# Two reorderings in a hybrid decoder layer: the differences of the second MLP weights two behind a product, and the first small products of head 0 twenty multiplications later

## The chip, the cores and the metric

The kernel runs on one core of one Trainium2 chip. The metric is the device time of one execution in microseconds (us). Before the change it is 1800.55 us, the median of three timed runs (1799.66, 1800.55 and 1804.9).

## The reference

One decoder layer in float32, sequence 1024, width 1024. A token mixer runs two branches side by side, sliding-window attention and a gated delta rule with eight heads; both are gated, added, projected and normalized. A squared-ReLU MLP with 4096 hidden channels follows. The parts that the change touches:

```python
u2 = x * (1.0 + sc2) + sh2
h = jnp.square(jax.nn.relu(u2 @ w_ff1[l] + b_ff1[l]))
x = _layer_norm(ALPHA * x + (1.0 + gt2) * (h @ w_ff2[l] + b_ff2[l]), ln2_g[l], ln2_b[l])
```

and, in the delta rule, for each head a triangular solve by chunks (`lax.linalg.triangular_solve(a_mat, rhs, ...)`), which the kernel does with an explicit inverse made of 64x64 blocks.

## The kernel before

**Numbers.** Every float32 factor of the large products is split into a high part (a copy on ScalarE, ACT, line 207) and a low part (raw minus high on VectorE, DVE, line 208). A product of two such factors takes three TensorE (PE) multiplications per block: high by high, high by low, low by high. One multiplication here is one MATMUL of 128x128 by 128x512.

**Order.** One list of events sets the order. `at(p, f)` puts a step at position p, where a position counts the large multiplications issued so far; before each multiplication all steps due by its position are emitted, those of equal position in the order in which they were put in. `after(n, f)` means n multiplications after the present one. PE, DVE and ACT run what was emitted in exactly that order. An engine doesn't wait for a position: it runs its next instruction as soon as its inputs are there and its output is free. POOL (GpSimd) and SP only issue DMAs in the stages below; their order is set by the framework.

**First MLP product.** It starts at position F0. The 2x2 blocks of `u2 @ w_ff1` are made with seven products instead of eight (names 1 to 7, table PROD), for 16 pairs of weight columns, i = 0 to 15. One product is 12 multiplications, so that 112 products make 1344 multiplications (line 2206). From pair 6 on a pair's order is 1, 2, 6, 5, 7, 3, 4. Products 1, 6, 7 and 4 add into one PSUM bank (tag `mm`; for pairs 3 and 4 tag `b`). After products 1 and 6 ACT copies the bank out (line 1920); after product 7 DVE adds it to a tile in SBUF (`full`, line 1389, emitted one multiplication after the product's end), and product 4 may not write to the bank before that has ended. Between product 7 and product 4 lies only product 3 (from pair 6 on; in the first pairs another one of 12 multiplications).

**What else DVE does there.** For each pair it makes sums and differences of the first weights (`f_sums`, `f_sums2`: tiles `x` and `fraw`), the low parts `wl` and `wd` (line 208), sums of the hidden activations (`h_sums`, `h_sums2`: tiles `sa`, `t` and `sb`), and the `full` additions (`t<-t,mm`, `t<-t,a`, `t<-t,b`).

**Differences of the second weights.** The second MLP product uses the same scheme, and needs four differences of blocks of `w_ff2` for each of 16 pairs n. `t_load(n)` issues three loads on POOL, 40 positions ahead (lines 2024 to 2026): into both halves of a tile `one`, into the first half of a tile `two`, and into one half of a tile `sb`. These tiles are single: the loads for pair n + 1 wait until pair n's results have been written out. `t_make(n)` at `F0 + MAKE[n]` does four subtractions on DVE in a row (tiles `wx`, `wx`, `wx`, `sb`; 128x512 each) and issues four DMAs on POOL that write the results to DRAM (line 2036). They are read again in the second MLP product, the last stage (multiplications of line 2266).

**Head 0.** The delta rule's heads start with `hd_load(h)` at position `early`, which loads the head's data; for head 0 it also issues `hd_solved(0)`: four loads on SP (lines 1140, 1141) into the single tiles `L21` and `T1`. `hd_z(0)` is eight PE products of 64x64 of these two tiles (line 1186) and a copy of the result to `Z` on ACT (line 1187). `hd_solved(1)` then loads head 1's blocks into the same two tiles, so that these four loads, on SP, wait for the products of `hd_z(0)`. `hd_x(0)` uses `Z` (line 1196) and is followed at once by `hd_z(1)`, which needs head 1's `L21` and `T1`.

Of the kernel before, what the change touches and what calls it, by code (L numbers as in the profile page):

```python
# [34 lines left out]
def hybrid_layer_kernel(ctx: ExitStack, tc: tile.TileContext,  # L35
                        x, c, w_ada, b_ada, w_in, conv_w, a_log, dt_bias, sinks, dn_norm_w,
                        w_oa, w_ob, w_out, ln1_g, ln1_b, w_ff1, b_ff1, w_ff2, b_ff2,
                        ln2_g, ln2_b, out, dbg=None):
    nc = tc.nc
    x, c, out = x[0], c[0], out[0]  # L40
# [6 lines left out]
    V, A, G, T = nc.vector, nc.scalar, nc.gpsimd, nc.tensor  # L47
# [40 lines left out]
    wt_d = dram.tile([4, D_FF // (2 * P), P, HALF], F32, name="wt_d")  # L88
# [100 lines left out]
    def at(p, f, *args):  # L189
        order[0] += 1  # L190
        heapq.heappush(events, (p, order[0], f, args))

    def after(n, f, *args):
        at(count[0] + n, f, *args)
# [357 lines left out]
    with tc.tile_pool(name="pa", bufs=2, side="right") as pa:  # L552
        if True:
            ba = pv.tile([P, NT, 16], F32, name="ba")
            for t in range(NT):
# [14 lines left out]
                if t:  # L570
                    vd = pa.tile([P, 4, 64], F32, tag="vd", name="vd", bufs=1)
                    a, b = (vraw, pv4) if t % 2 == 0 else (pv4, vraw)
# [101 lines left out]
        for h in range(8):  # L674
# [7 lines left out]
            for half in range(2):  # L682
                tp = psum("c", 1) if half else psum("b", 2)
                for j in range(4):
                    n = 4 * half + j
                    T.transpose(tp[:, j * P:(j + 1) * P], kT[:, n * P:(n + 1) * P], ident)
                for j in range(4):
                    n = 4 * half + j
# [16 lines left out]
            for half in range(2):  # L705
                kk = psum("a", 2)
                for j in range(4):
                    n = 4 * half + j
                    kc = kT[:, n * P:(n + 1) * P]
                    T.matmul(kk[:, j * P:(j + 1) * P], lhsT=kc, rhs=kc, start=True, stop=True)  # L710
                for j in range(4):
                    n = 4 * half + j
# [646 lines left out]
    for h in range(8):  # L1359
        R = R0 + PER * h  # L1360
        early = max(R - 118, OPEN + 1)
        at(early, hd_load, h)
        for half in range(2):
            at(R - 45 + 15 * half, hd_kq, h, half)
            at(R - 40 + 15 * half, hd_qturn, h, half)
            at(R - 10 + 15 * half, hd_vturn, h, half)
            at(R + (122 + 8 * half if h < 7 else 100 + 5 * half), hd_silu, h, half)
        if h == 0:
            at(early + 50, hd_z, 0)
            at(early + 52, hd_solved, 1)  # L1370
        at(R - 55 if h else R0 - 30, hd_x, h)
        at(R + 35, hd_gate, h)
        for n in range(NT):
            at(R + 3 * HOP * n, hd_a, h, n)
            at(R + 3 * HOP * n + HOP, hd_b, h, n)
            at(R + 3 * HOP * n + 2 * HOP, hd_c, h, n)
        at(R + PER + 2, hd_norm, h)
        at(R + PER + (45 if h < 7 else 29), hd_out, h, 0)
        at(R + PER + (60 if h < 7 else 33), hd_out, h, 1)
# [5 lines left out]
    def sub(E, out, a, b):  # L1385
        E.tensor_tensor(out=out, in0=a, in1=b, op=ALU.subtract)
# [256 lines left out]
    F0 = E0 + 4 * SEG  # L1643
# [313 lines left out]
    def half_s(j):  # L1957

        if "s" not in sums_:
            sums_["s"] = big2.tile([P, 2, HALF], F32, tag="l7", name="sb")  # L1960
        return sums_["s"][:, j]
# [30 lines left out]
    for i in range(1, NPAIR):  # L1992
        if i < EARLY:
            b = pos[i, 5]
# [6 lines left out]
        else:  # L2001
            b = pos[i, 1]
# [25 lines left out]
    def t_make(n):  # L2028
        one, two = wpair[n]
        t1, t2, t3, t4 = one[:, 0], two[:, 0], two[:, 1], half_s(1)  # L2030
        sub(V, t1, one[:, 1], t1)
        sub(V, t3, t2, one[:, 1])
        sub(V, t2, t2, t1)
        sub(V, t4, t4, t2)
        for j, t in enumerate((t1, t2, t3, t4)):
            nc.gpsimd.dma_start(out=wt_d[j, n], in_=t)

    MAKE = (172, 246, 320, 394, 484, 552, 620, 693, 767, 842, 916, 990, 1068, 1139, 1214, 1288)
    for n in range(NPAIR):
        at(F0 + MAKE[n] - 40, t_load, n)  # L2040
        at(F0 + MAKE[n], t_make, n)

# [146 lines left out]
    for i, m in seq:  # L2191
# [8 lines left out]
        for k in range(4):  # L2200
            for x_ in range(3):
# [3 lines left out]
                a, b = ((wh, uh_), (wh, ul_), (wl, uh_))[x_]  # L2205
# [139 lines left out]
```

## Time and profile before

| | before |
|---|---|
| timed runs, median of 3 | 1800.55 us (1799.66 to 1804.9) |
| profiled execution | 1801.69 us |
| its span, first to last instruction | 1800.0 us |
| PE busy | 99% of the span |
| DVE, ACT, POOL busy | 72%, 58%, 18% |
| granted TensorE clock, mean | 0.998 |
| DMA, mean | 195 GB/s |

All times in rows are from one profiled execution, in us from its first instruction. A row of the timeline gives start, duration, engine, line, operation, output and inputs, the count of merged instructions, and in brackets how long the engine stood idle just before and what released it. A busy share of 99% does not say that PE is at its peak: multiplications are pipelined, each is shown for 0.39 us, and the next starts 0.23 us after it. What an idle gap costs is therefore read from the starts of neighbouring multiplications.

### The profile page before, as it was taken

To read this page: it belongs to the slowest core of one execution; us is meant where nothing else is said; L and a number is where in the kernel's file an instruction comes from. 1 tells how busy PE (TensorE), PEld (TensorE's weight loads), DVE (VectorE), ACT (ScalarE), POOL (GpSimd) and SP (SyncE) were. 2 spreads that over 40 slices of the span, in tenths; PEclk is the share of its full clock that TensorE was granted. 3 is DMA by queue.
4 is the path that set the end of the run, shared out by engine and by line. 5 is a ranking of instruction groups with operands and counts; after the bars stand their busy time and mean duration, and the time that the engine had idled before them with its cause. 6 is when DMAs were issued, how large, how long until landed. Compare 5 with 4: busy or idle time off the path is not lost.

```text
span 1800.0 us, 26327 instructions
## 1 busy us (share of the span) xinstructions
PE 1781.7 (99%) x9134; PEld 1499.0 (83%) x9134; DVE 1303.5 (72%) x2411; ACT 1043.1 (58%) x2368; POOL 323.6 (18%) x478
## 2 busy tenths in 40 slices
PE   8999999999999999999999999999999999999998
PEld 6888888888888888888888888888888888888887
DVE  7677688988855576766687455888777766676697
ACT  4699678888865565655474341475555454434341
POOL 0333234554331011111002210002122120000000
PEclk9999999999999999999999999999999999999999
DMA  9555822232256565665747644359888889665571
GB/s 329 169 202 195 227 77 90 66 106 78 79 206 192 160 171 171 172 184 179 237 154 274 203 130 164 129 189 324 291 284 270 279 289 392 236 192 184 207 260 47
DMA packets 254295, 350.32 MB, mean 195 GB/s; under 512 B 26345, under 2 KB 158130, under 8 KB 253906
## 3 DMA queue, kind: packets, MB, share of 16 engines
q1 hardware_dynamic: 212146, 220.78, 38.4%
q0 software_dynamic: 31488, 106.85, 17.6%
q10 hardware_dynamic: 10528, 21.00, 3.2%
q8 instruction: 72, 1.18, 0.3%
q14 instruction: 61, 0.50, 0.1%
HBM read 238.74 MB, written 107.75 MB: 192 GB/s over the span
## 4 chain that ended last, share of the span: by engine, by line
PE 84%; ACT 5%; DVE 4%; DMA 2%; issue 1%; POOL 1%; ACTq 0%; SPq 0%; DVEq 0%; POOLq 0%
PE mm L250 33%; PE mm L2206 8%; PE mm L2266 7%; PE a L2266 4%; PE b L2206 4%; PE b L2266 4%; PE a L2206 3%; PE mm L1611 2%; PE c L2266 2%; PE c L933 2%; PE mm L1835 1%; PE b L1611 1%; PE a L859 1%; PE a L858 1%; PE a L1835 1%
## 5 line engine op out<-in xcount | busy, mean ns | idle before, releaser
L250 PE MATMUL mm<-uh,wh 128*128 128x512 f32 x800 | 319.7, 400 | 0.0
L250 PE MATMUL mm<-uh,wl 128*128 128x512 f32 x800 | 319.6, 400 | 0.0
L250 PE MATMUL mm<-ul,wh 128*128 128x512 f32 x800 | 318.8, 399 | 0.0
L208 DVE TENSOR_TENSOR sp<-sraw,sp 128x1024 fp32r<-128x1024 f32 x112 | 132.8, 1220 | 75.6 <-ACT sp L207 75.4
L207 ACT ACTIVATE sp<-sraw 128x1024 fp32r<-128x1024 f32 x112 | 112.6, 1053 | 121.0 <-PE b L2266 75.4
L250 PEld LDWEIGHTS mm<-uh,wh 128*128 128x128 f32 x800 | 150.7, 188 | 26.3 <-issue 0.2
L250 PEld LDWEIGHTS mm<-ul,wh 128*128 128x128 f32 x800 | 150.8, 188 | 26.0
L250 PEld LDWEIGHTS mm<-uh,wl 128*128 128x128 f32 x800 | 150.8, 188 | 26.0
L2266 PE MATMUL mm<-sp 128*128 128x512 f32 x528 | 135.9, 389 | 0.0
L2266 PEld LDWEIGHTS mm<-sp 128*128 128x128 f32 x528 | 98.8, 188 | 20.3
L2266 PE MATMUL a<-sp 128*128 128x512 f32 x336 | 92.2, 389 | 0.0
L1282 ACT ACTIVATE vn<-a,brk 128x128 f32<-128x128 f32 x64 | 23.6, 369 | 110.9 <-PE a L1280 110.9
L866 DVE CUSTOM_DVE_ANT_0 nscore<-a,amask,nsink 128x256 f32<-128x256 f32 (+1 forms) x128 | 54.4, 462 | 37.9 <-PE a L859 37.6
L225 DVE TENSOR_TENSOR wl<-wr,wh 128x1024 fp32r<-128x1024 f32 x56 | 72.7, 1298 | 11.2 <-ACT wh L221 11.0
L2266 PE MATMUL b<-sp 128*128 128x512 f32 (+1 forms) x336 | 79.6, 374 | 0.0
L877 POOL TENSOR_TENSOR sm<-sm 128x256 f32<-128x256 f32 x56 | 56.4, 1007 | 105.2 <-ACT sm L873 80.1
L2266 PEld LDWEIGHTS a<-sp 128*128 128x128 f32 x336 | 63.1, 188 | 13.1
L2266 PEld LDWEIGHTS b<-sp 128*128 128x128 f32 x336 | 60.3, 188 | 11.2
L208 DVE TENSOR_TENSOR wl<-fraw,wh 128x1024 fp32r<-128x1024 f32 x43 | 52.5, 1222 | 19.7 <-ACT wh L207 19.6
L207 ACT ACTIVATE wh<-fraw 128x1024 fp32r<-128x1024 f32 x43 | 44.9, 1055 | 31.0 <-PE b L2206 25.0
L873 ACT ACTIVATE sm<-nscore,stat 128x257 f32<-128x257 f32 (+1 forms) x128 | 61.9, 487 | 1.0 <-DVE stat L866 0.8
L756 DVE TENSOR_TENSOR stt<-M 128x62 f32<-128x62 f32 (+30 forms) x62 | 58.8, 949 | 2.7 <-issue 2.4
(566 smaller groups left out, 4737.1 us busy)
## 6 DMA issues: line engine op xcount, KB each, us to landing
wr<-in_w_in_dram SPq DMA_DIRECT2D x60, 512.0 KB, 3.6
sraw<-hf_d SPq DMA_DIRECT2D x54, 512.0 KB, 3.8
adaw<-in_w_ada_dram SPq DMA_DIRECT2D x83, 256.0 KB, 5.2
fraw<-in_w_ff_dram SPq DMA_DIRECT2D x32, 512.0 KB, 5.3
sraw<-wt_d SPq DMA_DIRECT2D x32, 512.0 KB, 4.3
hf_d<-t ACTq DMA_DIRECT2D x48, 256.0 KB, 4.3
wt_d<-wx POOLq DMA_DIRECT2D x48, 256.0 KB, 4.1
sraw<-in_w_ff_dram SPq DMA_DIRECT2D x22, 512.0 KB, 4.8
```

What stands on the lines that cost most here:

```text
L207: A.activation(out=hi, in_=src, func=AF.Copy)
L208: after(lag, lambda: V.tensor_tensor(out=lo, in0=src, in1=hi.bitcast(F32), op=ALU.subtract))
L225: V.tensor_tensor(out=hl[1], in0=raw, in1=hl[0].bitcast(F32), op=ALU.subtract)
L250: T.matmul(ts[half], lhsT=w[:, k, :], rhs=xx[k][:, sl], start=k == 0 and m == 0, stop=k == KT - 1 and m == 2)
L756: V.tensor_tensor(out=tv, in0=bc(M[:, 0:s, s:s + 1], [P, s, w]), in1=bc(M[:, s:s + 1, s + 1:64], [P, s, w]), op=ALU.mult)
L866: V.tensor_tensor_reduce(out=ns[:, i, 1:1 + W], in0=sc[:, i * 2 * P:i * 2 * P + W], in1=amask[:, mo:mo + W], scale=-1.0, scalar=nsink[:, 2 ...
L873: A.activation(out=sm[:, i, 0:1 + W], in_=ns[:, i, 0:1 + W], func=AF.Exp, scale=-1.0, bias=st[:, i:i + 1], accum_out=st[:, 2 + i:3 + i])
L877: G.tensor_tensor(out=sm[:, :, 1 + P:1 + 2 * P], in0=sm[:, :, 1:1 + P], in1=sm[:, :, 1 + P:1 + 2 * P], op=ALU.add)
L933: T.matmul(av[:, 0:256], lhsT=vt[:, b, :], rhs=p_[:, m, :], start=p_ is full and m == 0, stop=p_ is prods[-1][1] and m == 1)
L1611: T.matmul(pt, lhsT=t[:, lw, k, :], rhs=r[:, k % 2, :], start=begin and k == 0 and x_ == 0, stop=k == 3 and x_ == 2, skip_group_check=True)
L2206: T.matmul(pt, lhsT=a[:, kk, :], rhs=b[k], start=begin and k == 0 and x_ == 0, stop=k == 3 and x_ == 2, skip_group_check=True)
L2266: T.matmul(to, lhsT=a[:, f, t * P:(t + 1) * P], rhs=b[:, f, lo:up], start=(begin or own) and s % NS == 0 and f == 0 and x_ == 0, stop=s % ...
```

## The change

Two things move, and nothing is added or left out.

1. The four subtractions of `t_make` become two groups of two. The first group (`t1`, `t3`) is emitted two multiplications behind the end of a product, the second (`t2`, `t4`) twelve later, again two behind the end of a product. Each subtraction is followed by its own write to DRAM. `MAKE` stays, and is rounded: 172 becomes 170, 246 becomes 242, 394 becomes 398, 1068 becomes 1070. `t_load` stays where it was.
2. `hd_z(0)` is emitted at `early + 70` in place of `early + 50`. `hd_solved(1)` stays at `early + 52`, so that it now stands ahead of it.

```diff
         if h == 0:
-            at(early + 50, hd_z, 0)
+            at(early + 70, hd_z, 0)
             at(early + 52, hd_solved, 1)
@@
     def t_make(n):
         one, two = wpair[n]
         t1, t2, t3, t4 = one[:, 0], two[:, 0], two[:, 1], half_s(1)
-        sub(V, t1, one[:, 1], t1)
-        sub(V, t3, t2, one[:, 1])
-        sub(V, t2, t2, t1)
-        sub(V, t4, t4, t2)
-        for j, t in enumerate((t1, t2, t3, t4)):
-            nc.gpsimd.dma_start(out=wt_d[j, n], in_=t)
+        for j, (t, a, b) in enumerate(((t1, one[:, 1], t1), (t3, t2, one[:, 1]), (t2, t2, t1), (t4, t4, t2))):
+            after(12 * (j // 2), t_one_sum, n, (0, 2, 1, 3)[j], t, a, b)
+
+    def t_one_sum(n, j, t, a, b):
+        sub(V, t, a, b)
+        nc.gpsimd.dma_start(out=wt_d[j, n], in_=t)
...
         at(F0 + MAKE[n] - 40, t_load, n)
-        at(F0 + MAKE[n], t_make, n)
+        at(F0 + (MAKE[n] + 4) // 12 * 12 + 2, t_make, n)
```

The order on DVE at weight pair n = 12, before the change. `wx<-wx x3` and `sb<-sb,wx` are the four subtractions; `t<-t,mm` is the addition after product 7 of column pair 12, for which product 4 waits:

```order
L1386 TENSOR_TENSOR fraw<-fraw 128x512 x2
L208 TENSOR_TENSOR wl<-fraw,wh 128x1024
L1386 TENSOR_TENSOR wx<-wx 128x512 x3
L1386 TENSOR_TENSOR sb<-sb,wx 128x512
L1389 TENSOR_TENSOR t<-t,mm 128x512
L208 TENSOR_TENSOR wd<-x,wd 128x512
L1389 TENSOR_TENSOR t<-t,b 128x512
L208 TENSOR_TENSOR wl<-fraw,wh 128x1024
```

The same place in the changed kernel:

```order
L1386 TENSOR_TENSOR fraw<-fraw 128x512 x2
L208 TENSOR_TENSOR wl<-fraw,wh 128x1024
L1389 TENSOR_TENSOR t<-t,mm 128x512
L1386 TENSOR_TENSOR wx<-wx 128x512 x2
L208 TENSOR_TENSOR wd<-x,wd 128x512
L1389 TENSOR_TENSOR t<-t,b 128x512
L1386 TENSOR_TENSOR wx<-wx 128x512
L1386 TENSOR_TENSOR sb<-sb,wx 128x512
L208 TENSOR_TENSOR wl<-fraw,wh 128x1024
```

All four subtractions stood ahead of `t<-t,mm`; now none does.

The order on DVE at n = 3, among the first column pairs, as a piece of the difference. `t<-t,b` is the addition for which product 4 of column pair 4 waits:

```order
 L1386 TENSOR_TENSOR fraw<-fraw 128x512 x2
 L1386 TENSOR_TENSOR sb<-t,sa 128x512
-L1386 TENSOR_TENSOR wx<-wx 128x512 x3
+L1389 TENSOR_TENSOR t<-t,a 128x512
+L1386 TENSOR_TENSOR wx<-wx 128x512 x2
+L1389 TENSOR_TENSOR t<-t,b 128x512
+L1386 TENSOR_TENSOR wx<-wx 128x512
 L1386 TENSOR_TENSOR sb<-sb,wx 128x512
-L1389 TENSOR_TENSOR t<-t,a 128x512
-L1389 TENSOR_TENSOR t<-t,b 128x512
 L208 TENSOR_TENSOR wd<-x,wd 128x512
```

Four subtractions stood ahead of both additions; now none stands ahead of the first of them, and two ahead of the second.

The order on DVE at n = 8, before the change. `sa<-t`, `t<-t`, `sa<-t` are `h_sums` of column pair 8, `x<-fraw` and the three `fraw` rows behind it the sums of the first weights:

```order
L1386 TENSOR_TENSOR wx<-wx 128x512 x3
L1386 TENSOR_TENSOR sb<-sb,wx 128x512
L1386 TENSOR_TENSOR sa<-t 128x512
L1389 TENSOR_TENSOR t<-t 128x512
L1386 TENSOR_TENSOR sa<-t 128x512
L208 TENSOR_TENSOR wl<-fraw,wh 128x1024
L1386 TENSOR_TENSOR sb<-t,sa 128x512
L1389 TENSOR_TENSOR t<-t,a 128x512
L1386 TENSOR_TENSOR x<-fraw 128x512
```

The same place in the changed kernel:

```order
L1386 TENSOR_TENSOR sa<-t 128x512
L1389 TENSOR_TENSOR t<-t 128x512
L1386 TENSOR_TENSOR sa<-t 128x512
L208 TENSOR_TENSOR wl<-fraw,wh 128x1024
L1386 TENSOR_TENSOR wx<-wx 128x512 x2
L1386 TENSOR_TENSOR sb<-t,sa 128x512
L1389 TENSOR_TENSOR t<-t,a 128x512
L1386 TENSOR_TENSOR wx<-wx 128x512
L1386 TENSOR_TENSOR sb<-sb,wx 128x512
L1386 TENSOR_TENSOR x<-fraw 128x512
```

The subtractions stood ahead of `h_sums`; now they stand behind them and the `wl` row, and all four still ahead of `x<-fraw`.

On PE the eight products of `hd_z(0)` stand twenty large multiplications later, and on ACT the copy to `Z` stands behind one more `pad` copy, `vT` copy and `vT` activation. On SP the four loads of `hd_solved(1)` keep their place among the other DMAs; they wait for those eight products, as before. The order on POOL is the same.

## The prediction

> **What bounds the kernel now.** I read the page's totals first, then what PE waits for, then the timeline at those places.
>
> ```profile
> PE 1781.7 (99%) x9134; PEld 1499.0 (83%) x9134; DVE 1303.5 (72%) x2411; ACT 1043.1 (58%) x2368; POOL 323.6 (18%) x478
> ```
>
> PE is busy 99% of the span, so work that moves on DVE, ACT or the queues is worth what PE's waiting on it costs, no more. The waits of PE in the first MLP product (1155 to 1480 us), with what it waited for, total, times and longest:
>
> ```profile
> PE mm L2206 <- DVE t L1389: 0.8, 1, 0.8
> PE b L2206 <- DVE t L1389: 0.5, 1, 0.5
> PE c L2206 <- ACT t L1920: 0.2, 1, 0.2
> PE c L2206 <- DVE wl L208: 0.2, 1, 0.2
> ```
>
> Two waits for the addition `t` on DVE, two small others, and nothing else in 300 us. What the two cost is read from the starts of multiplications; undisturbed, 24 take 5.44 us, 0.227 each. Here is the multiplication ahead of each wait and the one that waited, for the first also the next:
>
> ```profile
> 1220.18 5.44 PE mm L2206 x24
> 1274.19 0.39 PE L2206 MATMUL mm<-u11h,wl 128*128 128x512 f32 x1
> 1275.10 0.50 PE L2206 MATMUL b<-mh,wh 128*128 128x512 f32 x1 [0.52 <-DVE t L1389]
> 1275.44 0.39 PE L2206 MATMUL b<-ml,wh 128*128 128x512 f32 x1
> 1424.92 0.39 PE L2206 MATMUL b<-u22h,wl 128*128 128x512 f32 x1
> 1426.11 0.50 PE L2206 MATMUL mm<-mh,wh 128*128 128x512 f32 x1 [0.80 <-DVE t L1389]
> ```
>
> First wait: 1275.44 - 1274.19 = 1.25 for two steps that take 0.45, 0.80 lost, of which 0.11 in the step behind the one that waited. Second: 1426.11 - 1424.92 - 0.23 = 0.96, with the same 0.11 behind it 1.07 lost. DVE just ahead of each addition:
>
> ```profile
> 1271.11 2.01 DVE L1386 TENSOR_TENSOR wx<-wx 128x512 f32<-128x512 f32 x3
> ...
> 1274.36 0.68 DVE L1389 TENSOR_TENSOR t<-t,b 128x512 f32<-128x512 f32 x1
> ...
> 1422.72 2.01 DVE L1386 TENSOR_TENSOR wx<-wx 128x512 f32<-128x512 f32 x3
> 1425.38 0.68 DVE L1389 TENSOR_TENSOR t<-t,mm 128x512 f32<-128x512 f32 x1
> ```
>
> Both times DVE runs the four subtractions in a row (three in 2.01, the fourth as long as the others, 2.7 in all) while the addition that PE is about to need stands behind them. These are n = 3 and n = 12.
>
> **The subtractions, where PE waited.** At n = 12 none of them stands ahead of `t<-t,mm` any more: it can start where they did, at 1422.72 (product 7 ended 12 multiplications, 2.7 us, before 1424.92 + 0.23 = 1425.15, where product 4 would start undisturbed), and be done at 1423.4. The 1.07 go. At n = 3, `t<-t,a` and two subtractions stand ahead of `t<-t,b`: from 1271.11, 0.7 + 1.4 + 0.7 end at 1273.9, before 1274.19 + 0.23 = 1274.42. The 0.80 go. Together 1.87.
>
> **The subtractions, where PE did not wait.** The number of instructions is the same, only their order on DVE changes, so the question is which addition now comes late. Of the sixteen places one worries me, n = 8, where the subtractions move behind `h_sums`:
>
> ```profile
> 1351.18 2.01 DVE L1386 TENSOR_TENSOR wx<-wx 128x512 f32<-128x512 f32 x3
> 1354.99 0.69 DVE L1386 TENSOR_TENSOR sa<-t 128x512 f32<-128x512 f32 x1 [1.08 <-ACT t L1929]
> 1360.84 1.42 DVE L1386 TENSOR_TENSOR fraw<-fraw 128x512 f32<-128x512 f32 x2
> 1364.46 1.23 DVE L208 TENSOR_TENSOR wl<-fraw,wh 128x1024 fp32r<-128x1024 f32 x1 [2.21 <-ACT wh L207]
> 1365.60 0.68 DVE L1389 TENSOR_TENSOR t<-t,mm 128x512 f32<-128x512 f32 x1
> ...
> 1363.38 1.05 ACT L207 ACTIVATE wh<-fraw 128x1024 fp32r<-128x1024 f32 x1
> ...
> 1368.03 0.39 PE L2206 MATMUL mm<-mh,wh 128*128 128x512 f32 x1
> ```
>
> Before, the four ran while DVE had nothing else (it then stood idle 1.08 for ACT). Now `sa` still starts at 1354.99, and the four come between it and `fraw`, which ends 2.7 later, at 1362.26 + 2.7 = 1364.96. ACT's `wh` needs it: 1364.96 to 1366.0. Then `wl` (1365.60 - 1364.46 = 1.14 to the next), then `t<-t,mm`, done at 1367.8 to 1367.9. PE needs it at 1368.03. So the cover of 2.2 us of idle is used up and some 0.15 is left; that everything here comes 0.8 earlier after n = 3 moves both alike. If a step takes a little longer it costs 0 to 0.3; I take 0.1. At the other places the additions that PE waits for have as few subtractions ahead of them as before, or fewer, or DVE idles between.
>
> **The reload.** The tiles are single, so the later second group delays the next pair's loads, and its first group on DVE would wait for them, with everything on DVE queued behind. Worst from n = 8 to 9. The first two rows are the time from issue to landing (shortest, median, longest) of n = 8's writes and of the reload of `two`; the third is the instruction that stood behind n = 9's subtractions:
>
> ```profile
> DMA to landing us min/median/max: 4.7/5.0/5.3
> DMA to landing us min/median/max: 6.2/6.2/6.2
> 1374.04 0.69 DVE L1386 TENSOR_TENSOR sa<-t 128x512 f32<-128x512 f32 x1 [1.05 <-ACT t L1929]
> ```
>
> `t2` of n = 8 ends at about 1361.3, its write lands at 1366.4, the reload at 1372.6. DVE would wait inside the first group of n = 9, and finish it at 1373.3, before `sa` at 1374.04; the second group now stands behind `sa`. I cost the reload at nothing; what covers it is the 1.05 of idle ahead of `sa` and the time that the second group took there; each DMA 1 us slower, and `sa` and all behind it come 1.3 late. The Trainium skill ("SBUF — State Buffer", section "SBUF: two separate sides") says more against the change: a DMA issued from GpSimd can't write its descriptors while DVE holds the shared port. By that rule the second group's write and reload would each wait out a DVE instruction beside them, about 1.2 us each, and land near 1375. The trace speaks against it: two writes of n = 3, issued while DVE ran the subtractions and additions quoted above without a break, landed after 2.3 to 2.5, sooner than those of n = 8:
>
> ```profile
> L2036 POOL DMA_DIRECT2D wt_d<-wx x2: 545/545/545, 1272.1 to 1272.7; - x2
> ...
> DMA to landing us min/median/max: 2.3/2.4/2.5
> ```
>
> **Head 0.** PE's products of `hd_z(0)`, SP's first and last load of head 1, PE's products that need those loads, then the share of DMA (next to last column) in two stretches; last, time to landing of one of the four, and of one of head 2's four, issued 12 us later:
>
> ```profile
> 555.12 0.68 PE L1186 MATMUL b<-T,L 64*64 64x64 f32 x16
> 555.85 0.54 SPq L1140 DMA_DIRECT2D L<-l_d  x1
> 559.50 0.61 SPq L1141 DMA_DIRECT2D T<-t_d  x1
> 567.38 0.63 PE L1186 MATMUL b<-T,L 64*64 64x64 f32 x16
> 555.00:562.00 7.00, 7.00 (x49) 5.89 (x49) 2.26 (x3) 3.23 (x6) 0.00 (x0) 1.00 1.06 337
> 562.00:568.00 6.00, 6.00 (x62) 5.11 (x60) 5.33 (x13) 2.33 (x11) 0.14 (x1) 1.00 0.29 72
> ...
> DMA to landing us min/median/max: 7.7/7.7/7.7
> ...
> DMA to landing us min/median/max: 2.2/2.2/2.2
> ```
>
> PE did not wait at 555.12, so moving the products gains nothing in this execution (at most the 0.1 by which they start late). Twenty multiplications are 4.5 us. The four loads wait for the products, so SP now issues the first at 560.4 and the last three issues later: 1.8 at 0.6 each, 3.7 as slowly as here, so at 562.2 to 564.1; SP is held meanwhile, and its next DMA stood at 565.63. With 2.2 to landing the last is there by 566.3, with 7.7 as late as 571.8. PE wants them at 567.38: 0 to 4.4 us of waiting, 2.5 with 7.7 and the quick issue. I take 0, since DMA is at 0.29 in that stretch and the loads that crowded 555 to 562 were issued before. The Trainium skill ("DMA: Bandwidth & Descriptors", section "Issuing engines are not separate DMA queues") has transfers of all queues interleave on the same 16 engines; by it the 2.2 holds only if POOL's loads are through by then, else the sum rises by those 2.5. The two shares with their landings agree with the rule. ACT's copy to `Z` has 6 us to spare.
>
> **Sum.** Against the profiled execution, 1801.69 (1.69 around the span): -0.80 - 1.07 + 0.1 = -1.77, so 1799.9. The median of the timed runs is 1.14 below the profiled one: 1798.8.
>
> **Rivals.**
> *A, given back at the entry of the second product.* ACT waits there for loads, DVE splits behind it, and PE comes soon after (the second of the three multiplications, 1497.26, uses the low part):
>
> ```profile
> 1491.02 1.06 ACT L207 ACTIVATE sp<-sraw 128x1024 fp32r<-128x1024 f32 x1 [1.12 <-DMA sraw<-hf_d]
> 1495.36 1.22 DVE L208 TENSOR_TENSOR sp<-sraw,sp 128x1024 fp32r<-128x1024 f32 x1
> 1497.03 0.84 PE L2266 MATMUL mm<-sp 128*128 128x512 f32 x3
> ```
>
> If the loads land when they did, PE is there at 1495.5, the split ends at 1496.58, and 1.1 is given back: 1799.9. Against it: these loads are issued when PE and DVE release their tiles, which happens earlier too.
> *B, slower: head 1's loads come late.* 2.5 us of waiting for PE: 1801.3, slower than before; it decides from a last landing after 567.38 + 1.8 = 569.2, where it outweighs the gain. For it are the 7.7 and the full DMA up to 562.
> *C, the reload.* Writes and reloads 1 to 2 us slower than at n = 8 hold DVE up at n = 9 and at two or three other pairs, and each time the addition behind comes some 1 us late: 1801.8. For it is that 0.15 was left at n = 8; against it that most pairs lie further from their reload.
> *D, no effect.* The two waits belong to the profiled execution and the timed runs haven't got them: 1800.6.
>
> **Numbers.** Forecast 0.60, A 0.13, B 0.13, C 0.06, D 0.08. About 0.3% (5.4 us) can be told from no change. All five lie within it. Faster by more would need three times the waits that PE has here: 0.02. Slower by more needs B or C at well over double its price: 0.04. For the range: low is the forecast less 0.9, by which the fastest timed run is under the median, less the two small waits (0.4) and half a us for a wait at 555 that a timed run may have had, 1797.0; high is B plus that same 0.9, 1802.2.
>
> **What would show it.** In the profile after: no PE wait for DVE `t` L1389 near 1274 and 1424; at n = 8 the addition ends within 0.3 of product 4's start; DVE waits for DMA in `wx` at n = 9; SP's loads of head 1 from 560.4, landed before 567. It is wrong if PE waits for DMA at line 1186, if new waits for `t` stand at other pairs, or if the first multiplication of the second product isn't 1.8 earlier.

## The result and the profile after

| | before | changed |
|---|---|---|
| timed runs, median of 20 each | 1800.53 us | 1798.22 us |
| lowest and highest | 1799.2 and 1805.69 | 1797.12 and 1799.84 |
| mean | 1801.09 | 1798.29 |
| profiled execution, its span | 1801.69, 1800.0 | 1799.08, 1797.3 |

The ratio of the times is 0.9985, with a 95% interval of 0.9978 to 0.9992: a gain of 2.3 us, within the 0.3% that the prediction called no change. The kernel before has a tail that the changed one lacks: four of its twenty runs lie 2.9 to 5.2 us above its median.

What PE waits for in the first MLP product of the changed kernel (1155 to 1480 us; total, times, longest):

```profile
PE c L2206 <- DVE wl L208: 0.2, 1, 0.2
PE c L2206 <- ACT t L1920: 0.2, 1, 0.2
```

The two waits for `t` are gone and none took their place. PE at the three places and at the last product 4 (the multiplication ahead, and the first one that needs the addition):

```profile
1273.77 0.39 PE L2206 MATMUL mm<-u11h,wl 128*128 128x512 f32 x1
1274.00 0.39 PE L2206 MATMUL b<-mh,wh 128*128 128x512 f32 x1
...
1366.27 0.39 PE L2206 MATMUL b<-u22h,wl 128*128 128x512 f32 x1
1366.50 0.39 PE L2206 MATMUL mm<-mh,wh 128*128 128x512 f32 x1
...
1423.39 0.39 PE L2206 MATMUL b<-u22h,wl 128*128 128x512 f32 x1
1423.62 0.39 PE L2206 MATMUL mm<-mh,wh 128*128 128x512 f32 x1
...
1480.74 0.39 PE L2206 MATMUL mm<-mh,wh 128*128 128x512 f32 x1
```

DVE in the changed kernel, at n = 1, 3, 8, 9 and 12:

```profile
1233.71 0.69 DVE L1386 TENSOR_TENSOR wx<-wx 128x512 f32<-128x512 f32 x1 [0.61 <-DMA wx<-in_w_ff_dram]
...
1271.29 1.28 DVE L1386 TENSOR_TENSOR wx<-wx 128x512 f32<-128x512 f32 x2
1272.50 0.68 DVE L1389 TENSOR_TENSOR t<-t,b 128x512 f32<-128x512 f32 x1
...
1365.53 0.68 DVE L1389 TENSOR_TENSOR t<-t,mm 128x512 f32<-128x512 f32 x1
...
1368.71 1.29 DVE L1386 TENSOR_TENSOR wx<-wx 128x512 f32<-128x512 f32 x2
...
1421.19 0.68 DVE L1389 TENSOR_TENSOR t<-t,mm 128x512 f32<-128x512 f32 x1
1421.79 1.28 DVE L1386 TENSOR_TENSOR wx<-wx 128x512 f32<-128x512 f32 x2
```

Read the two fences against each other: the end of an addition, and how long after it PE starts. At n = 3 it ends at 1273.18, 0.82 ahead of PE; at n = 12 at 1421.87, 1.75 ahead; at n = 8 at 1366.21, 0.29 ahead. PE's steps at these places are 0.23, the undisturbed pitch. The last product 4 starts at 1480.74, where in the kernel before the same multiplication stood at 1483.43: 2.69 earlier, and the span is 2.7 shorter. All but 0.03 of it is still there at the last multiplication of the kernel.

The 2.69 are made up so: 0.42 was there before the first MLP product began (PE's waits near the start of the program, for a load, differ from execution to execution by several tenths). 2.27 arose in the product: the 1.87 of the prediction, 0.22 in two steps near 1284 (0.34 each before, 0.23 now; DVE's `wl` there had been done only 0.06 ahead of PE, now 1.11), and 0.18 in steps that differ too little to be named.

Head 0 in the changed kernel: PE's products of `hd_z(0)` and of `hd_z(1)`,

```profile
559.14 0.68 PE L1186 MATMUL b<-T,L 64*64 64x64 f32 x16
...
566.85 0.63 PE L1186 MATMUL b<-T,L 64*64 64x64 f32 x16
```

SP's first and last load of head 1 and its next DMA,

```profile
559.86 0.53 SPq L1140 DMA_DIRECT2D L<-l_d  x1
...
562.11 0.61 SPq L1141 DMA_DIRECT2D T<-t_d  x1
565.10 0.39 SPq L125 DMA_DIRECT2D wr<-in_w_in_dram  x1
```

and the time to landing of the load that was issued at 561.12, the last but one:

```profile
DMA to landing us min/median/max: 2.7/2.7/2.7
```

That one is there at 563.8, 3 us ahead of `hd_z(1)`; the last, a us behind it, made nobody wait.

### The profile page after: what moved, and what is told of

Same layout as the page of the kernel before. It is cut to its first block, busy times and chain, and to the rows that moved or that the text cites. A ratio compares the mean times of both kernels' runs of the same rounds, so it can differ in the third digit from the quotient of the medians.

```text
span 1797.3 us, 26326 instructions
## 1 busy us (share of the span) xinstructions
PE 1781.3 (99%) x9134; PEld 1499.2 (83%) x9134; DVE 1301.2 (72%) x2411; ACT 1044.1 (58%) x2368; POOL 323.3 (18%) x478
## 4 chain that ended last, share of the span: by engine, by line
PE 88%; ACT 5%; DVE 3%; DMA 1%; issue 1%; POOL 0%; SPq 0%; ACTq 0%; DVEq 0%; POOLq 0%
PE mm L250 33%; PE mm L2206 8%; PE mm L2266 7%; PE a L2266 4%; PE b L2206 4%; PE b L2266 4%; PE a L2206 3%; PE mm L1611 2%; PE mm L1835 2%; PE c L2266 2%; PE c L933 2%; PE a L1835 1%; PE b L1611 1%; PE a L859 1%; PE a L858 1%; PE c L1304 1%
```

## The experiments

Each was timed beside the kernel before on the same chip; that kernel's median was 1800.72 us for the first four, 1800.93 for the next four and 1801.59 for the last four, so differences from it are compared rather than times.

**1. The MLP part alone** (of the changed kernel):

```diff
-            at(early + 70, hd_z, 0)
+            at(early + 50, hd_z, 0)
```

> The regrouped subtractions alone; the products of head 0 stay at early + 50. If the subtractions carry the whole gain, the time is that of the changed kernel, about 1798.3 us, 2.2 below the kernel before, and PE has no wait for DVE t L1389. If head 0 has a part in it, it stays 0.5 us or more above the changed kernel. If the few slow executions of the kernel before (3 of 20 at 1803.4 or more) come from head 0's loads, some of this kernel's executions are that slow as well.

Measured: 1798.47 us, 2.25 less than the kernel before, ratio 0.9986 (0.9977 to 0.9995). Its PE waits in the first MLP product are the same two of 0.2. The MLP part makes the whole gain of the median. None of its 11 runs is more than 2.0 over that median, though `hd_z(0)` stands at its old place: the late runs that were expected if head 0's loads cause them did not show here. The kernel before had only two of 27 on this chip, so that 11 runs decide little.

**2. The head part alone** (of the kernel before):

```diff
-            at(early + 50, hd_z, 0)
+            at(early + 70, hd_z, 0)
```

> The products of head 0 twenty multiplications later, alone; the subtractions stay as they were. If head 0 costs and gives nothing, the median is that of the kernel before, 1800.5 us, with the two PE waits for DVE t L1389 of 0.5 and 0.8 us still there. If it gives part of the gain, 0.5 us or more below. If the slow executions come from head 0's loads, none of this kernel's executions is above 1802.

Measured: 1800.51, ratio 0.9998 (0.9989 to 1.0007). The median doesn't move. But none of its 11 runs is more than 1.0 over its median, while the kernel before had two more than 4.7 over it among 27. At two in 27, some four of ten such samples of 11 runs would have none by chance, so this alone doesn't show that the head part takes the tail away.

**3. Only the two pairs that wait** (of the kernel before; the four subtractions stay in a row, at n = 3 and n = 12 they go behind the addition):

```diff
-    MAKE = (172, 246, 320, 394, ..., 1068, ...)
+    MAKE = (172, 246, 320, 410, ..., 1070, ...)
```

> From the kernel before, only the subtractions of n = 3 and n = 12 are put behind the addition that PE waits for (MAKE 394 becomes 410, 1068 becomes 1070); all stay four in a row and the other fourteen stay where they were. If what counts is solely what stands ahead of these two additions, this gives the whole gain: 1798.3 to 1798.7 us. If making two groups of all sixteen matters, it gains less, with 1799.5 or more.

Measured: 1798.57, 2.15 less, ratio 0.9989 (0.9980 to 0.9998). Two numbers of the table bring what the whole MLP part brings; at the other fourteen pairs it did nothing for the median. The traces say the same more sharply: from the start of the first to that of the last multiplication of the first MLP product it is 309.88 us before, 307.61 in the changed kernel, 307.61 in experiment 1, 309.91 in experiment 2 and 307.66 here. In this execution PE did wait at `hd_z(0)`:

```profile
PE b L1186 <- DMA T<-t_d: 0.3, 1, 0.3
```

**4. The subtractions put ahead of more additions** (of the kernel before):

```diff
+    MAKE = (172, 246, 320, 394, 480, 564, 630, 693, 767, 842, 916, 984, 1068, 1152, 1236, 1300)
```

> From the kernel before, the four subtractions are put directly ahead of the addition t<-t,mm at five more pairs (n = 4, 5, 11, 13, 14), as they are at n = 12. If subtractions ahead of that addition are what PE waits for, each adds a wait of about 1.1 us, n = 4 about 1.9, in all 6 us: 1806.5 us, with seven waits of PE for DVE t L1389. If the two waits of the kernel before were accidents of their place, the time stays within 1 us of 1800.5.

The edit also moves n = 6 and n = 15, by 10 and 12 multiplications; there the four don't stand directly ahead of the addition after product 7.

Measured: 1810.09, ratio 1.0052 (1.0039 to 1.0065). The waits for `t` came, at each of the seven pairs at which four subtractions stood directly ahead of the addition (n = 3, 4, 5, 11, 12, 13, 14):

```profile
PE mm L2206 <- DVE t L1389: 5.6, 6, 1.6
PE b L2206 <- DVE t L1389: 0.5, 1, 0.5
```

The sign and the place were right, the size was 3.6 too small. Following the starts of the same multiplications through both traces, the first MLP product lost 6.6 us against the kernel before, near the 6 that had been summed; two places that the sum had left out lost the rest (the part ahead of `hd_z(0)` was 1.1 quicker in this execution). At the entry of the second product PE waits for `sp` on DVE (1.8 lost); DVE idles there for ACT, and ACT for a load, as is shown under rival A below. And at `hd_z(0)`, which had not been touched, PE waited for its load (2.2 lost):

```profile
PE b L1186 <- DMA T<-t_d: 2.0, 1, 2.0
```

In experiments 3 and 4 the second `T` load of head 0 was issued at 544.42 and 543.52, and PE's wait for it ended at 555.5 and 556.2, 11.1 and 12.7 later. In the trace of before the same load had landed within 10.5, since PE didn't wait. That gave a theory for the tail (theory H): this landing varies, and the head part covers it.

**5. hd_z(0) earlier:**

```diff
-            at(early + 70, hd_z, 0)
+            at(early + 30, hd_z, 0)
```

> The changed kernel with hd_z(0) 40 multiplications (9.1 us) earlier than it put it, so 20 earlier than before had it. In two of the traces with the old place (the third and the fourth experiment) PE waited 0.3 and 2.0 us at line 1186 for the second T load of head 0, which landed 11.1 and 12.7 us after its issue, at 555.5 and 556.2; in the other two it did not wait. Theory H, that this landing differs from execution to execution and that the tail of the kernel before (6 of 47 runs 2.9 us or more over the median) is PE waiting for it: PE reaches the products at about 550.1 and waits in every execution, 0.6 at least (the two loads whose landing is recorded came at 549.3 to 551.2) and 3 to 6 where the last load is as late as in those two; the median is 1799.5 to 1803 and the runs spread over 3 us or more. Rival, that the tail comes from elsewhere and the loads all land near 550.8: a wait of 0.5 to 1.0, median 1798.7 to 1799.3, runs within 2.7 us as in the changed kernel.

Measured: 1802.95 us, but with runs from 1798.96 to 1810.62. Theory H gave the median and the spread; the rival's 2.7 of spread is far off. PE in the profiled execution, which is the slowest of the runs:

```profile
552.75 0.44 PE L1186 MATMUL b<-T,L 64*64 64x64 f32 x2 [3.34 <-DMA T<-t_d]
557.21 1.08 PE L1186 MATMUL b<-T,L 64*64 64x64 f32 x14 [4.03 <-DMA T<-t_d]
558.22 0.79 PE L250 MATMUL mm<-uh,wh 128*128 128x512 f32 x1
558.82 0.63 PE L250 MATMUL mm<-ul,wh 128*128 128x512 f32 x1
559.24 0.63 PE L250 MATMUL mm<-uh,wl 128*128 128x512 f32 x1
```

The second `T` load, issued at 543.36, let PE go at 557.2: 13.8 us. And the multiplications behind the wait are 0.43 apart, not 0.23. The granted clock says why (the number after POOL's; then DMA share and GB/s):

```profile
549.00:553.00 4.00, 0.66 (x4) 0.28 (x2) 3.09 (x4) 1.86 (x3) 0.69 (x2) 0.96 1.01 385
553.00:557.00 4.00, 0.19 (x2) 0.00 (x0) 0.30 (x1) 0.00 (x0) 0.00 (x0) 0.50 1.04 325
...
560.00:562.00 2.00, 2.00 (x6) 1.52 (x5) 0.00 (x0) 0.00 (x0) 0.00 (x0) 0.50 0.45 103
562.00:564.00 2.00, 2.00 (x9) 1.59 (x8) 0.00 (x0) 0.00 (x0) 0.00 (x0) 0.77 0.77 213
564.00:568.00 4.00, 4.00 (x19) 3.31 (x18) 0.59 (x1) 1.18 (x2) 0.00 (x0) 1.00 0.11 31
```

After the idle stretch the clock is 0.50 until some 5 us after PE has resumed. From 558.22 eleven steps took 4.79 instead of 2.50, another 2.3 us on top of the 7.4 of waiting.

Counted over all runs: with `hd_z(0)` at its old place, 21 of the 117 runs of the kernel before lie more than 2.5 us above the median of their comparison (and 1 of 27 runs of experiments 1, 3 and 4). With it at the new place none of 91 does (the changed kernel and experiments 2 and 8 to 12); the highest is 2.1 above. Experiment 7, at the new place too, has one of 12, 2.9 above, among waits of its own.

How far this goes: experiment 5 moves `hd_z(0)` alone and makes late runs, so this wait can make such a tail. That it makes the tail of the kernel before is likely and not shown. The share of late runs differs from chip to chip: two of 27 in the comparison of experiments 1 to 4, ten of 35 in the last one, where none of the 48 runs at the new place is late. And 80 of the 91 runs carry the changed MLP part too; it begins some 600 us behind `hd_z(0)`, which speaks against it as the cause.

**6. hd_z(0) later:**

```diff
-            at(early + 70, hd_z, 0)
+            at(early + 84, hd_z, 0)
```

> The changed kernel with hd_z(0) 14 further multiplications later. SP's loads of head 1 now stand behind its next weight load, at 565.1, so they are issued from about 565.7 to 568; with 2.5 to 2.7 from issue to landing as in the changed kernel the last is there at 570.6. PE wants them near 567.4. Rival B of the prediction, which was put at a point too early: PE waits 2.5 to 3.5 us at line 1186 for DMA and the time is 1800.7 to 1801.7, slower than the changed kernel, no faster than the one before. If head 1's loads are hidden wherever they stand: no wait there and 1798.0 to 1798.6.

Measured: 1802.90 (1801.57 to 1804.69), 2.0 more than the kernel before, ratio 1.0006 (0.9998 to 1.0014). SP's loads now run from 564.94 to 566.85, and PE waits for them, in an execution that is one of the fastest of this kernel:

```profile
568.76 1.08 PE L1186 MATMUL b<-T,L 64*64 64x64 f32 x16 [1.58 <-DMA T<-t_d]
```

So rival B exists, with `hd_z(0)` at 563.87 instead of 559.14. The wait in this execution is smaller than the 2.5 to 3.5 expected, and the median is 1.2 over the upper end of what was expected; this profile, at 1801.63, can't show where the others lose more. Five of the twelve runs list a mean granted clock of 0.997, and none of the 35 runs of the kernel before beside them does, so that a part of it may be the clock (see the last section).

**7. The second group 24 multiplications behind the first:**

```diff
-            after(12 * (j // 2), t_one_sum, n, (0, 2, 1, 3)[j], t, a, b)
+            after(24 * (j // 2), t_one_sum, n, (0, 2, 1, 3)[j], t, a, b)
```

> The changed kernel with the second two subtractions 24 instead of 12 multiplications behind the first two, so that each pair's reload starts 2.7 us later. In the changed kernel the reload stood 0.5 to 2.3 us ahead of its first use at n = 2, 5, 6, 9, 10, 11 and 0.6 behind it at n = 1. Rival C (the reload): DVE waits for DMA in wx at six or more pairs, 6 to 12 us in all, the additions behind come late, PE waits 1 to 4 us for t, and the time is 1799.2 to 1802. My theory, that the additions have 0.8 to 1.7 us of slack behind such a wait: DVE's waits come, 5 to 12 us, PE's waits for t stay under 0.7 and the time is 1797.9 to 1799.0.

Measured: 1803.01, ratio 1.0011 (1.0002 to 1.0019). My theory fell: the slack doesn't cover a reload that starts 2.7 us later. The time is also 1.0 over the upper end that rival C had. DVE's waits for the reload came as both had it,

```profile
DVE wx L1386 <- DMA wx<-in_w_ff_dram: 9.3, 7, 3.0
```

but PE waits too (1155 to 1510 us):

```profile
PE c L2206 <- DVE wl L208: 1.9, 2, 1.7
PE mm L2266 <- DVE sp L208: 1.1, 2, 0.8
PE mm L2266 <- ACT sp L207: 0.4, 1, 0.4
PE mm L2206 <- DVE t L1389: 0.3, 1, 0.3
```

The longest is at n = 1, where what is queued behind the waiting subtraction is not only an addition but the split `wl`. On DVE the wait, and the split that PE wanted:

```profile
1237.05 0.69 DVE L1386 TENSOR_TENSOR wx<-wx 128x512 f32<-128x512 f32 x1 [3.02 <-DMA wx<-in_w_ff_dram]
...
1245.22 1.22 DVE L208 TENSOR_TENSOR wl<-fraw,wh 128x1024 fp32r<-128x1024 f32 x1
```

PE there:

```profile
1246.50 0.50 PE L2206 MATMUL c<-mh,wl 128*128 128x512 f32 x1 [1.68 <-DVE wl L208]
```

This is rival C with its mechanism, at a place that the prediction hadn't named, and with the `wl` of the next product rather than `t`. The other large loss is at the entry of the second product (2.4 us); it follows a late load, and whether the later reloads make that load late is open (see rival A below).

**8. The first of the two waits that are left** (of the changed kernel):

```diff
-    at(F0 + 92, f_beta, 0)
+    at(F0 + 78, f_beta, 0)
```

> The changed kernel with the split f_beta(0) 14 multiplications earlier (at F0+78, in a stretch in which ACT idles 2.6 us), for the two waits of PE that are left in the first MLP product, at 1205.8 (for wl, 0.39 lost) and at 1211.3 (for ACT's t, 0.37 lost). Theory: both go, the time is 0.4 to 0.75 lower than that of the changed kernel, 1797.5 to 1797.9. Rival: the split delays ACT's mh, which PE needs for the same products, and the loss only moves: 1798.0 to 1798.8. For the tail this is 11 more runs with hd_z(0) at its new place: none more than 2.0 over the median by theory H.

Measured: 1798.94, ratio 0.9984 (0.9975 to 0.9992). The wait for `wl` went, and the next one took its place:

```profile
PE c L2206 <- ACT t L1920: 0.7, 1, 0.7
```

The rival was right in the place, and the time is 0.1 over its upper end: PE is at that multiplication 0.4 earlier, ACT's `t` isn't.

**9. The new places alone** (of the changed kernel, four in a row):

```diff
         for j, (t, a, b) in enumerate(((t1, one[:, 1], t1), (t3, t2, one[:, 1]), (t2, t2, t1), (t4, t4, t2))):
-            after(12 * (j // 2), t_one_sum, n, (0, 2, 1, 3)[j], t, a, b)
+            sub(V, t, a, b)
+        for j, t in enumerate((t1, t2, t3, t4)):
+            nc.gpsimd.dma_start(out=wt_d[j, n], in_=t)
```

> The changed kernel with the four subtractions of each pair in a row again, at the new places: the change without its 12 multiplications between the pairs. At n = 12 they stand behind t<-t,mm; at n = 3 all four stand behind t<-t,a, but still ahead of t<-t,b. Theory (what counts is how many subtractions stand ahead of the addition that PE needs): n = 12 is free, at n = 3 PE waits 0.4 to 0.7 for t (0.6 to 0.9 lost, since t<-t,a and four subtractions take the same 4.0 us in either order), so 1798.6 to 1799.3. Rival: the new place alone does it all: no such wait, 1798.0 to 1798.5.

Measured: 1799.49, ratio 0.9984 (0.9975 to 0.9992). The wait at n = 3 is there (line 2206 is 2208 in this kernel), with 0.8 lost, and none at n = 12:

```profile
PE b L2208 <- DVE t L1389: 0.5, 1, 0.5
```

**10. The two groups alone, at the old places** (of the changed kernel):

```diff
-        at(F0 + (MAKE[n] + 4) // 12 * 12 + 2, t_make, n)
+        at(F0 + MAKE[n], t_make, n)
```

> The changed kernel with the first two subtractions at their old places (F0 + MAKE[n]) and the other two 12 multiplications later: the change without its new places. At n = 12 two of them stand ahead of t<-t,mm, at n = 3 two ahead of t<-t,a and two more between it and t<-t,b. Theory: at n = 12 the addition ends at 1422.7 + 1.4 + 0.7 = 1424.8 in the times of the kernel before, 0.35 ahead of PE, so no wait; at n = 3 0.4 to 0.7 of waiting remain (0.6 to 0.9 lost): 1798.6 to 1799.3. Rival: two halves ahead of an addition are as bad as four, n = 12 waits 0.3 or more as well: 1799.4 to 1800.4. Second rival: the split alone does it all, 1798.0 to 1798.5.

Measured: 1799.67, ratio 0.9981 (0.9972 to 0.9991). The same picture, again at n = 3 alone:

```profile
PE b L2206 <- DVE t L1389: 0.4, 1, 0.4
```

Both come out 0.2 to 0.4 over the expected times, on a chip whose kernel before is 1.1 over that of the first comparison; against experiment 11, which has no such wait and ran beside them, they are 0.5 and 0.7 slower. At n = 12 either half of the change is enough; n = 3 needs both.

**11. The second group 18 multiplications behind the first:**

```diff
-            after(12 * (j // 2), t_one_sum, n, (0, 2, 1, 3)[j], t, a, b)
+            after(18 * (j // 2), t_one_sum, n, (0, 2, 1, 3)[j], t, a, b)
```

> The changed kernel with 18 multiplications between the two halves; 12 gave 1798.2 with one DVE wait of 0.6 us for the reload, 24 gave 1803.0 with seven, 9.3 us in all. Theory (rival C decides between them by the reload, which starts 1.36 us later than in the changed kernel): DVE waits for DMA in wx at two to five pairs, 2 to 5 us in all, PE loses 0.3 to 1.5 us at n = 1 (waiting for wl behind it) and some at the entry of the second product: 1798.6 to 1800.6. If the loss at 24 came from the order on DVE and not from the reload, DVE's waits for DMA would grow like this and the time would stay within 1797.9 to 1798.6.

Measured: 1798.97, ratio 0.9982 (0.9973 to 0.9991). DVE waits at one pair instead of two to five, longer than in the changed kernel:

```profile
DVE wx L1386 <- DMA wx<-in_w_ff_dram: 2.1, 1, 2.1
```

It is n = 1 again. `wl` ends at 1244.17 there, and PE:

```profile
1243.84 0.39 PE L2206 MATMUL c<-ml,wh 128*128 128x512 f32 x1
1244.22 0.50 PE L2206 MATMUL c<-mh,wl 128*128 128x512 f32 x1
1244.56 0.40 PE L2206 MATMUL c<-mh,wh 128*128 128x512 f32 x1
```

Steps of 0.38 and 0.34 instead of 0.23, 0.26 lost: the cover is just used up. Another 6 multiplications, and experiment 7's waits begin. The theory had more waits of DVE and 0.3 to 1.5 of loss; it was right in the place. The time alone doesn't settle it against the order on DVE as the cause, since the loss is small; the traces do, as far as n = 1 goes: DVE runs the same order there with 12, 18 and 24 multiplications, waits 0.6, 2.1 and 3.7 for the reload, and `wl` behind it ends later by as much (1243.1, 1244.2, 1246.4).

**12. Both remaining waits** (of the changed kernel):

```diff
-    at(F0 + 92, f_beta, 0)
+    at(F0 + 78, f_beta, 0)
...
-    at(pos[0, 5] + 10, f_delta, 0)
+    at(pos[0, 5] + 14, f_delta, 0)
```

> The changed kernel with f_beta(0) 14 multiplications earlier, as in the eighth run, and f_delta(0) 4 later, so that ACT's t<-c stands ahead of its wd and starts 0.5 us earlier. In the eighth run the first of the two remaining waits went and the second grew from 0.2 to 0.7. Theory: now both shrink to 0.25 or less in all, 0.3 to 0.7 us less than the changed kernel in its profile, 1797.5 to 1798.1 beside a kernel before of 1800.6. Rival: the wait moves on once more, to wd or mh: within 0.3 of the changed kernel.

Measured: 1798.18 beside a kernel before of 1801.59, ratio 0.9974 (0.9964 to 0.9984). One wait is left in the first MLP product:

```profile
PE c L2206 <- ACT t L1920: 0.2, 1, 0.2
```

So the theory held. It is 0.8 faster than experiment 11 beside it, and its span is 0.8 shorter than that of the changed kernel, of which 0.45 come from the wait that went and the rest from the start of the program. The intervals of the two overlap, so that it is faster than the changed kernel is likely and not shown; it is faster than the kernel before.

## Why the prediction was right, point by point

**The two waits, -1.87.** Right in place and size. Experiments 1 and 3 show that the two pairs make the gain of the median, experiment 4 that the mechanism (four subtractions ahead of the addition that frees PE's bank) makes PE wait 0.5 to 1.6 us at each of the seven pairs at which it stands. The prediction missed 0.22 near 1284, where the trace of before showed no wait because the two slow steps stood under what is listed.

**n = 8, 0.1.** The margin was told as 0.15 and is 0.29; it cost nothing.

**The reload, 0.** Right in the sum, wrong in the working. It put DVE's wait at n = 9; the only one is 0.61 at n = 1. The step that failed is the transfer time, taken from n = 8 of before (5.0 for the writes, 6.2 for the reload). The same DMAs in the changed kernel, issued 1357 to 1367, from issue to landing:

```profile
DMA to landing us min/median/max: 2.3/2.8/4.5
```

The last reload into `wx` was issued at

```profile
1362.86 0.54 POOL L2025 DMA_DIRECT2D wx<-in_w_ff_dram  x1 [1.01 <-DMA wt_d<-wx]
```

and so was there by 1367.4, ahead of its first use at 1368.71. DVE ran from 1353.46 to 1363.26 without a break while these writes were issued and landed, so the 1375 that the prediction worked out by the rule of the Trainium skill ("SBUF — State Buffer", section "SBUF: two separate sides") did not come about here either. The prediction read that rule too widely: the section ties the lockout of descriptor writing to DVE operations in a two-port mode, and says of operations with two SBUF inputs, as these subtractions are, that they lock only against a GpSimd operation that reads SBUF. The risk itself was real and nearer than told: experiment 11 shows that 1.4 us more just uses up the cover, and experiment 7, with 2.7 us more, is 2.1 us slower than the kernel before, though only its losses at n = 1 (1.9) and at the last addition (0.7) are shown to come from the reload.

**Head 0, 0.** The 2.2 to landing was the right one to take (2.5 to 2.7 measured), and PE doesn't wait. But "moving the products gains nothing in this execution" was carried over to the timed runs with half a us in the lower bound alone. The one profiled execution had no wait there; some one in six of the timed runs of that kernel lie 2.6 to 6 us over the median, and such a wait is the likely cause. The landing of head 0's own loads was the term to bound, and the highest of the three runs shown, 4.35 over their median, was the only sign of it. That the tail is gone moves the mean (2.8 us gained) more than the median (2.3).

**Sum and median.** Against the profiled execution -2.61 instead of -1.77: the 0.1 not paid, 0.40 more in the first MLP product, 0.42 ahead of it that the change has no part in, and 0.08 less behind it and around the span. That the 0.42 helped the changed kernel's profile is luck. The median came 0.6 under the predicted 1798.8 and within its range.

**Rivals.** A, given back at the entry of the second product: no, the lead of 2.69 there is 2.66 at the end. The place is tight all the same, and the trace names what rival A named, a load. ACT's third copy `sp` for the second product reads a load from `hf_d`; here it is in the changed kernel, 3.8 us ahead of the product's first multiplication (1483.46), and in experiment 5, 1.9 behind it (1493.08):

```profile
1479.67 1.07 ACT L207 ACTIVATE sp<-sraw 128x1024 fp32r<-128x1024 f32 x1 [1.41 <-DMA sraw<-hf_d]
...
1494.94 1.06 ACT L207 ACTIVATE sp<-sraw 128x1024 fp32r<-128x1024 f32 x1 [2.82 <-DMA sraw<-hf_d]
```

In ten of the fourteen traces it starts 0.6 to 4.9 ahead, and the second product takes at most 0.4 more than in the kernel before. In experiments 10, 4, 5 and 7 it starts 0.6, 1.6, 1.9 and 2.3 behind, and the product takes 0.8, 1.8, 2.0 and 2.4 more. The order on DVE isn't what decides, since experiment 5 has that of the changed kernel there. Why the load is late in these four is open. B, head 1's loads: not at the new place, but 4.7 us behind it (experiment 6). C, the reload: not with 12 multiplications, with 24 (experiment 7). D, no effect: no, by experiments 1 and 3.

## What to carry to other kernels

Where one engine is busy all the time, look for the instruction that it waits for and count what stands ahead of that one on its engine: moving two groups of four subtractions behind two additions gained as much as rearranging all sixteen. A wait that the profiled execution doesn't show can still be in the timed runs: a tail in their times, and a load that lands just ahead of its use, are the hint, and a use some 4 us later left no late run among 91 here. Before work is pushed back to free an engine, follow the buffers that it holds to their next load, at every pair: the place that decides is the one with the least cover, here the pair n = 1 and not the one that looked busiest.

## What the runs showed of the hardware

**The same load lands at very different times.** The second `T` load of head 0, issued in the same order of work, with DMA near its full share, let PE go within 10.5 us of its issue in the trace of before and 11.1, 12.7 and 13.8 us after it in three others (experiments 3, 4 and 5). Of the first `T` load of head 0 every trace has the landing: 6.3 (experiment 9) to 10.5 us (experiment 5) after its issue.

**A wait of PE costs more than itself once it is long.** The wait of 2.0 us in experiment 4 left the granted clock at 1.00; the two of experiment 5, 3.3 and 4.0 us with two small products between them, brought it to 0.50 for some 10 us, 5 of them after PE had resumed, and 2.3 us on top. The Trainium skill ("TensorE: Matmul & The Clock Gate", section "What's actually happening") says the same: an idle window of some 3.4 us halves the clock, a busy one of that length brings it back. The trace agrees with the first and shows a longer return, which a window that runs freely allows. That the large numbers of the tail have this share in them is possible: in the last comparison seven of the ten late runs of the kernel before list a mean granted clock of 0.996 or 0.997, and its other 25 runs 0.998 or 0.999. On the two chips before it the late runs list 0.998 or 0.999 like the others, and no late run of that kernel was profiled.
